# First stage of a two-layer hybrid trunk: the modulation beside the first column tiles, ordered anew

## The chip, the cores and the metric

The kernel runs on one core of one Trainium2 chip. The metric is the device time of an execution in microseconds (us), as a median over runs. Engines: TensorE (PE, its weight loads PEld), VectorE (DVE), ScalarE (ACT), GpSimd (POOL) and SyncE (SP), which issues nearly all loads.

## What is computed

A trunk of two layers over 256 latent and 256 context tokens of 2048 features. Only the entry of layer 0 matters here: a normalised input, modulated per feature, then projected.

```python
shift, scale, gate = jnp.split(jax.nn.silu(c) @ w_mod + b_mod, 3, axis=-1)
shift_x, scale_x, gate_x = jnp.split(jax.nn.silu(c_ctx) @ w_mod + b_mod, 3, axis=-1)
z_lat = (rms_norm(h_lat, norm_g) * (1.0 + scale[:, None]) + shift[:, None]) @ w_in
z_ctx = (rms_norm(h_ctx, norm_g) * (1.0 + scale_x) + shift_x) @ w_in
```

Everything is float32. The branches behind `z` (a gated linear recurrence, a gated delta rule, attention), the output projection and layer 1 follow, and the change leaves them as they are.

## The kernel before, in words

Activations lie as 16 feature tiles `Y` of 128 features by 512 tokens. A projection is exact to about float32: each operand is split into a high and a low float32r part (`xh`, `xl` of the input, `wh`, `wl` of the weights), and every contraction step makes three products of 128 x 512 (`accumulate`, lines 391 to 395).

The first stage is `start_layer` (line 528) for layer 0. It keeps seven column tiles (`FIRST`) open in seven PSUM tiles `pz`, `pz`, `pa`, `pa`, `pb`, `pb`, `pt`, and goes through the 16 feature tiles as contraction steps: 21 products a step. Before feature tile k can be used, its shift and scale must be known. They come from `mod_narrow` (lines 218 to 249), a generator. For a feature tile it goes through eight chunks of 128 x 512 weights of `w_mod0`: four load by themselves into `wb`, `wb`, `wa`, `wb`, four in pairs into `full` (or, every second tile, `th`) and `kq`. A chunk is four products of a stationary operand of two columns (`cs`, the SiLU of the two conditions), each in a column group of 32 of its own (`tile_position`), summed over the chunks in `pm`. Then ScalarE copies `pm` into `s`, TensorE transposes it, and VectorE adds up two column groups each, with the bias, into `modS` and `modA`, and applies the gain (`scale_gain`): a copy and three instructions. `modulate` (line 336) then makes `u`, `xh` and `xl` of the tile, in two halves of 256 tokens (latent and context).

The generator is pulled by `advance` (line 535): 8 steps beside the sums of squares (`rms_bcast`), one, then `LEAD` = 14 steps ahead of the first product, and one or two behind each column tile of a step. Each pull that uses a chunk also issues its load on SP's queue.

```python
for i in sorted(range(NSTART), key=lambda i: wide(TILES[l][i][0])):
    wh, wl = first_w[k][i // 4]
    accumulate(first[i], wh, wl, P * (i % 4), k, TT if wide(TILES[l][i][0]) else T)
    advance(1 + (i in (1, 5)))
```

The code's order is not the built order: a scheduler places the instructions of each engine by its own account of when their operands are there. All loads wait in SP's queue, in order; `wb` has 8 buffers, `wa` and `kq` 4 and 2, `full` and `th` one each, raw weights `wraw` and their parts `wh`, `wl` four each. Names in the trace are those of the tiles; nearly all computation has line 90, where a helper records it.

Of the kernel before, what the change touches and what calls it, by code (L numbers as in the profile page):

```python
# [7 lines left out]
F32 = mybir.dt.float32  # L8
# [13 lines left out]
# column tiles of the input projection, 128 columns each, in the order they are computed  # L22
# [14 lines left out]
LEAD = 14  # L37
# [14 lines left out]
class Timed:  # L52
    """An engine, with a rough account of when the work given to it will be done."""
# [42 lines left out]
def trunk(ctx, tc, xT, cT, consts, masks, rope_t, small, fg, w_mod0, w_mod, w_first, w_in, w_ba, w_rg, w_out, out):  # L96
# [31 lines left out]
    nc.sync.dma_start(out=cst[:, 0:C_TRI], in_=consts[:, 0:C_TRI])  # L128
    ident = cst[:, C_ID:C_ID + P]
# [32 lines left out]

    sm = []
    for l in range(2):
        s = big.tile([P, S_END], F32, name=f"small{l}")
        sm.append(s)
    nc.sync.dma_start(out=sm[0], in_=small[0])
# [50 lines left out]
    def mod_narrow():  # L218
        """Shift and scale of layer 0, one tile of features after the other; yields None, or the tile that is done."""
        pm = psum("pm", bufs=1)  # L220
        dve.memset(pm, 0.0)
        for u in range(KT):
            o = T * (u % 2)
            for j in range(8):
                if j < 4:
                    wm = tmp("wa" if j == 2 else "wb")
                    nc.sync.dma_start(out=wm, in_=w_mod0[u, j])
                else:
                    if j % 2 == 0:
                        tag = "kq" if j == 6 else ("full", "th")[u % 2]  # L230
                        two = tmp(tag, (P, 2, TT), bufs=BUFS.get(tag, 1))
                        nc.sync.dma_start(out=two, in_=w_mod0[u, j:j + 2].rearrange("j p c -> p j c"))
                    wm = two[:, j % 2]
# [3 lines left out]
                if j < 7:  # L237
                    yield None
            mt = tmp("s", (P, P))
            act.copy(out=mt, in_=pm[:, o:o + P])  # L240
            yield None
# [18 lines left out]
    def mod_step(engine=None):  # L260
        """One chunk of 256 x 512 weights: products on TensorE, or sums on VectorE with TensorE at the end."""
# [93 lines left out]
    def split(a, hi=None, lo=None):  # L355
        """The two float32r parts of a, in tiles of their own if no place is given."""
# [7 lines left out]
    def product3(out, a, b):  # L364
        """out = a.T @ b of two split operands."""
# [3 lines left out]
    class Weights:  # L369
        """Quarters (four of the sixteen contraction steps) of column tiles, in the order of their use."""  # L370
# [26 lines left out]
    def project(weights, ns, between):  # L397
        """One group of column tiles, with other work in between; returns their results in PSUM."""
# [28 lines left out]
    # depthwise convolution over the tokens of each segment; z in PSUM, token range [s0, s1) in halves  # L427
# [13 lines left out]
    # 2 silu(u), into dst  # L441
# [20 lines left out]
    class Background:  # L462
        """Lanes of work that runs between the projections, a step at a time, when its operands should be there."""
# [10 lines left out]
        def begin(self, makes, g):  # L474
            """The first step of a piece of work now, the others later."""
# [37 lines left out]
    def first_weights(l, k):  # L513
        raw = wp.tile([P, 1024], F32, tag="wraw", name="wraw", bufs=4)
        nc.sync.dma_start(out=raw[:, 0:P * NSTART], in_=w_first[l, k])
        first_w[k] = [split_w(raw[:, 0:512], 512), split_w(raw[:, 512:P * NSTART], P * NSTART - 512)]

    def gate_weights(l):
        """Columns of beta and alpha, split, of all contraction steps."""
# [8 lines left out]
    def start_layer(l, acc, bs, wide):  # L528
        """The layer's input, and with it, one contraction step after the other, its first column tiles."""
        first = [psum("pz"), psum("pz"), pa_(), pa_(), pb_(), pb_()]  # L530
        narrow = mod_narrow() if l == 0 else iter(())
        pr = rms_bcast(acc, TT, lambda: [mod_step(pe) if l else next(narrow, None) for _ in range(FILL if l else 8)])
        rb = tmp("wa")

        def advance(n):
            for _ in range(n):
                u = next(narrow, None)
                if u is not None:
                    modulate(l, u, rb)

        if l == 0:
            dve.tensor_copy(rb, pr)
            advance(1)
            first_weights(0, 0)
            advance(LEAD)
        else:
            modulate(l, 0, pr)
            dve.tensor_copy(rb, pr)
        first.append(pt_())
        for k in range(KT):  # L550
            if k + 1 < KT and k + 1 not in first_w:
                first_weights(l, k + 1)
            if l and k + 1 < KT:
                modulate(l, k + 1, rb)
            if l == 0 and k == 3:
                late_loads()
            for i in sorted(range(NSTART), key=lambda i: wide(TILES[l][i][0])):
                wh, wl = first_w[k][i // 4]
                accumulate(first[i], wh, wl, P * (i % 4), k, TT if wide(TILES[l][i][0]) else T)
                advance(1 + (i in (1, 5)))  # L560
# [3 lines left out]
    def layer(l, acc, bs):  # L564
# [8 lines left out]
        for dst, o in ((cq, 0), (sq_, T)):  # L573
            nc.sync.dma_start(out=dst, in_=rope_t[:, o:o + T])
            dve.tensor_scalar(out=dst, in0=dst, scalar1=s[:, S_QN:S_QN + 1], scalar2=None, op0=ALU.mult)
# [29 lines left out]
        def branch_result(k, src, cc, scale=None):  # L605
            """Columns cc of a branch's result, times half its gate if that is there."""
# [9 lines left out]
        def beta_alpha():  # L616
# [42 lines left out]
            # rows of the cumulated decay, to be read back on every partition  # L659
# [12 lines left out]
        # Keys stay as they come from the convolution; 1 / |k| of a token is carried by beta and v instead.  # L672
# [132 lines left out]
            # norm over the head's features, back to [feature, token]  # L805
# [414 lines left out]
```

## Time and profile before

| what | us |
|---|---|
| median of three runs (lowest, highest) | 1541.25 (1536.79, 1542.35) |
| span of the profiled execution (its own time is not listed beside it) | 1537.5 |
| TensorE busy | 1477.6 (96%) |
| VectorE busy | 1173.4 (76%) |
| ScalarE busy | 739.5 (48%) |
| three groups of products into `pz` | 642.5, 629.9, 629.8 |

The profile is one execution. Busy time of TensorE is that of pipelined products, whose ends are modelled, so starts that follow each other tell more than durations. In a row in order of time, the bracket behind an instruction is the idle time of its engine before it and what ended it. On TensorE and PEld a float32 product shows as two instructions, so a chunk of four products is x8.

### The profile page before, as it was taken

Reading aid. Unit: us, or ns where it says so; the run is one execution under the profiler, and the core shown is the slowest. Engines: PE = TensorE matmul, PEld = TensorE weight load, DVE = VectorE, ACT = ScalarE, POOL = GpSimd, SP = SyncE. Lnnn points to the kernel's source line nnn. Section 1 sums busy time; section 2 is a strip of 40 time slices with the busy share of each in tenths; the row PEclk is TensorE's granted clock in tenths of the full one; section 3 lists DMA queues with packets and bytes.
Section 4 is the critical chain, followed back from the end, with each engine's and each line's share of the span. In section 5 each row is a group of like instructions: output and inputs, shape, how many; then the busy total and the mean of one; then the engine's idle time right before and its main releaser. Section 6 shows DMA issues by size and latency. Waiting matters only on the chain.

```text
span 1537.5 us, 29960 instructions
## 1 busy us (share of the span) xinstructions
PE 1477.6 (96%) x11746; PEld 1200.2 (78%) x11746; DVE 1173.4 (76%) x2542; ACT 739.5 (48%) x1708; POOL 112.9 (7%) x114
## 2 busy tenths in 40 slices
PE   4999999999999999999999999999999999999996
PEld 2666768787877877788878887867977889779996
DVE  4444989898898898999748876787895676788755
ACT  3223445554444546655422224554644555677653
POOL 0000010100020010000011110010100100000011
PEclk9999999999999999999999998999999999999998
DMA  9996444343443463344436555544551333233553
GB/s 341 341 337 239 152 131 138 113 161 111 144 158 110 142 185 109 108 146 156 142 124 223 201 198 191 179 141 164 197 180 63 97 111 105 79 107 125 191 187 116
DMA packets 90686, 247.68 MB, mean 161 GB/s; under 512 B 9200, under 2 KB 20912, under 8 KB 90544
## 3 DMA queue, kind: packets, MB, share of 16 engines
q1 hardware_dynamic: 89392, 244.71, 47.7%
q8 instruction: 92, 1.51, 0.4%
q10 hardware_dynamic: 1152, 1.05, 0.2%
q14 instruction: 50, 0.41, 0.1%
HBM read 243.60 MB, written 2.13 MB: 160 GB/s over the span
## 4 chain that ended last, share of the span: by engine, by line
PE 80%; DVE 10%; DMA 4%; ACT 3%; issue 1%; POOL 1%; SPq 0%; DVEq 0%; POOLq 0%; ACTq 0%
PE pz L90 56%; PE pa L90 9%; PE pb L90 8%; PE pt L90 4%; PE pm L90 3%; DVE wb L90 2%; DVE wl L90 2%; DVE macc L90 1%; DVE th L90 1%; DMA wraw<-in_w_in 1%; DMA wa<-rows_d 1%; ACT wb L90 1%; DMA Y<-in_xT 1%; DVE u L90 1%; ACT t L90 1%
## 5 line engine op out<-in xcount | busy, mean ns | idle before, releaser
L90 PE MATMUL pz<-xh,wh 128*128 128x512 f32 (+1 forms) x1760 | 642.5, 367 | 1.7 <-ACT xh L90 1.7
L90 PE MATMUL pz<-xh,wl 128*128 128x512 f32 (+1 forms) x1760 | 629.9, 358 | 0.8 <-DVE wl L90 0.8
L90 PE MATMUL pz<-xl,wh 128*128 128x512 f32 (+1 forms) x1760 | 629.8, 358 | 0.0
L90 ACT CAST wh<-wraw 128x512 fp32r<-128x512 f32 x488 | 293.3, 612 | 335.8 <-PE pz L90 206.3
L90 DVE TENSOR_TENSOR wl<-wraw,wh 128x512 fp32r<-128x512 f32 x488 | 329.4, 683 | 135.7 <-ACT wh L90 133.4
L90 PEld LDWEIGHTS pz<-xl,wh 128*128 128x128 f32 x1760 | 331.8, 189 | 50.0 <-issue 3.1
L90 PEld LDWEIGHTS pz<-xh,wh 128*128 128x128 f32 x1760 | 331.9, 189 | 48.9 <-ACT xh L90 2.4
L90 PEld LDWEIGHTS pz<-xh,wl 128*128 128x128 f32 x1760 | 332.3, 189 | 42.4 <-DVE wl L90 1.2
L90 DVE SCALAR_TENSOR_TENSOR macc<-wm,cs,macc 128x512 f32<-128x512 f32 x400 | 293.3, 766 | 1.4 <-DMA wm<-in_w_mod 1.0
L90 PE MATMUL pb<-wb 128*128 128x128 f32 (+1 forms) x560 | 112.6, 328 | 3.6 <-ACT wb L90 1.9
L90 PEld LDWEIGHTS pb<-wb 128*128 128x128 f32 x560 | 79.6, 190 | 16.7 <-ACT wb L90 6.9
L90 POOL TENSOR_TENSOR o<-o,t 128x512 f32<-128x512 f32 (+1 forms) x28 | 30.5, 1091 | 326.2 <-ACT t L90 326.2
L90 ACT ACTIVATE wb<-pb,mx,rqa 128x512 f32<-128x512 f32 (+1 forms) x48 | 33.9, 707 | 42.6 <-DVE mx L90 42.3
L90 DVE SCALAR_TENSOR_TENSOR u<-zp,small,u 128x512 f32<-128x512 f32 (+1 forms) x72 | 50.6, 702 | 1.9 <-ACT u L90 1.7
L90 DVE COPY s<-pm 128x64 f32<-128x64 f32 x16 | 3.6, 225 | 62.5 <-PE pm L90 62.5
L90 ACT ACTIVATE xh<-u,modS 128x256 fp32r<-128x256 f32 x64 | 29.3, 502 | 45.1 <-DVE u L90 45.0
L90 ACT ACTIVATE t<-pt 128x128 f32<-128x128 f32 (+1 forms) x122 | 34.1, 280 | 32.0 <-PE pt L90 29.9
L90 PEld LDWEIGHTS pa<-c,s 32*32 32x32 f32 x2304 | 25.0, 107 | 21.7 <-issue 12.0
L90 ACT COPY s<-pm 128x128 f32<-128x128 f32 x16 | 4.3, 267 | 70.5 <-PE pm L90 70.5
L90 DVE TENSOR_REDUCE mx<-pb 128x1 f32<-128x512 f32 (+1 forms) x48 | 28.7, 599 | 10.3 <-PE pb L90 9.9
L90 POOL TENSOR_TENSOR rqa<-rqa,mhalf 128x4 f32<-128x4 f32 (+1 forms) x16 | 17.3, 1084 | 244.7 <-DVE rqa L90 244.7
L90 ACT COPY wb<-pb 128x512 f32<-128x512 f32 (+1 forms) x48 | 24.7, 515 | 21.7 <-PE pb L90 21.0
(259 smaller groups left out, 1812.7 us busy)
## 6 DMA issues: line engine op xcount, KB each, us to landing
wraw<-in_w_in SPq DMA_DIRECT2D x148, 512.0 KB, 3.6
wm<-in_w_mod SPq DMA_DIRECT2D x128, 512.0 KB, 3.6
wraw<-in_w_out SPq DMA_DIRECT2D x64, 512.0 KB, 4.2
wraw<-in_w_first SPq DMA_DIRECT2D x32, 448.0 KB, 4.6
wb<-in_w_mod SPq DMA_DIRECT2D x48, 256.0 KB, 5.6
kq<-in_w_mod SPq DMA_DIRECT2D x16, 512.0 KB, 5.1
Y<-in_xT SPq DMA_DIRECT2D x16, 256.0 KB, 5.3
wa<-in_w_mod SPq DMA_DIRECT2D x16, 256.0 KB, 5.7
```

The lines of the kernel that those rows point to most:

```text
L90: return f(*args, **kw)
```

## The change

`mod_narrow` becomes a class `Narrow` with three parts: `load` issues all six loads of a tile, `run` makes four of its chunks (after the second four also the copy to `s`), and `end` makes the sums. In `end` one product with a selection matrix `sel4` (128 x 4, a sum of columns of the identity) takes the place of the transposition, and two VectorE instructions with two scalars each write `modA` and `modS`. `pm` uses its first 128 columns for every tile.

`start_layer` for layer 0 becomes `start_first`. In the code, the second four chunks of tile k+1 stand behind the second column tile of step k, its sums behind the third, and the first four chunks of tile k+2 behind the sixth. Loads are issued as whole tiles, three steps ahead. The small parameters load ahead of `Y`; masks, the rope tables, the weights of beta and alpha and other small blocks (`late`) load in step 11 instead of the beginning and step 3. Layer 1 keeps its code.

```diff
@@ small parameters ahead of Y, the selection matrix
+    sm = [big.tile([P, S_END], F32, name=f"small{l}") for l in range(2)]
+    nc.sync.dma_start(out=sm[0], in_=small[0])
...
+    sel4 = big.tile([P, 4], F32, name="sel4")
+    for g in range(2):
+        dve.tensor_tensor(out=sel4[:, 2 * g:2 * g + 2], in0=ident[:, 32 * g:32 * g + 2], in1=ident[:, 64 + 32 * g:66 + 32 * g], op=ALU.add)
@@ mod_narrow becomes Narrow
+        def run(self, u, half):
+            for j in range(4 * half, 4 * half + 4):
                 for c in range(4):
-                    pe.matmul(out=pm[32 * c:32 * c + 2, o:o + P], lhsT=cs[:, 2 * j + c // 2, :], rhs=wm[:, c * P:c * P + P],
+                    pe.matmul(out=self.pm[32 * c:32 * c + 2, 0:P], lhsT=cs[:, 2 * j + c // 2, :], rhs=self.chunks[u][j][:, c * P:c * P + P],
                               start=(j == 0), stop=(j == 7), tile_position=(0, 32 * c))
...
-            pe.transpose(out=pm[:, o + P:o + 2 * P], in_=mt, identity=ident)
-            even = tmp("s", (P, P))
-            dve.tensor_copy(even[:, 0:64], pm[:, o + P:o + P + 64])
-            for g, dst in enumerate((modS[0], modA[0])):
-                dve.scalar_tensor_tensor(out=dst[:, u, :], in0=pm[:, o + P + 64 + 32 * g:o + P + 66 + 32 * g], scalar=sm[0][:, S_BM + 16 * g + u:S_BM + 16 * g + u + 1],
-                                         in1=even[:, 32 * g:32 * g + 2], op0=ALU.add, op1=ALU.add)
-            scale_gain(0, u, 1)
-            yield u
...
+        def end(self, u):
+            pe.matmul(out=self.pm[:, 0:4], lhsT=self.mt, rhs=sel4, start=True, stop=True)
+            dve.tensor_scalar(out=modA[0][:, u, :], in0=self.pm[:, 2:4], scalar1=self.one[:, u:u + 1], scalar2=sm[0][:, S_G + u:S_G + u + 1], op0=ALU.add, op1=ALU.mult)
+            dve.tensor_scalar(out=modS[0][:, u, :], in0=self.pm[:, 0:2], scalar1=sm[0][:, S_BM + u:S_BM + u + 1], scalar2=None, op0=ALU.add)
@@ start_first
+        for u in range(2):
+            narrow.load(u)
+            first_load(0, u)
+        pr = rms_bcast(acc, TT, lambda: narrow.run(0, 0))
+        rb = tmp("wa")
+        dve.tensor_copy(rb, pr)
+        narrow.run(0, 1)
+        narrow.end(0)
+        modulate(0, 0, rb)
+        first_split(0)
...
+        for k in range(KT):
+            for i in range(NSTART):
+                wh, wl = first_w[k][i // 4]
+                accumulate(first[i], wh, wl, P * (i % 4), k, TT)
+                if k + 1 == KT:
+                    continue
+                if k == 0 and i == 0:
+                    narrow.run(1, 0)
+                if i == 1:
+                    narrow.run(k + 1, 1)
+                    if k + 3 == KT - 1:
+                        first_load(0, k + 3)
+                    if k + 3 < KT:
+                        narrow.load(k + 3)
+                    if k + 3 < KT - 1:
+                        first_load(0, k + 3)
+                    first_split(k + 1)
+                if i == 2:
+                    narrow.end(k + 1)
+                    modulate(0, k + 1, rb)
+                if i == 5 and k + 2 < KT:
+                    narrow.run(k + 2, 0)
+            first_w.pop(k)
+            if k == KT - 5:
+                late()
```

The first place is TensorE in step 1, around the sums for tile 2 (`cst,s` is the transposition, `sel4,s` the selection product; `xh1`, `xl1` are the operand of step 1, `xh2` that of step 2). Before:

```order
L90 MATMUL pm_240<-kq_432,cs_107 2x128 x8
L90 MATMUL pz_222<-xl1_374,wh_414 128x512
L90 MATMUL pz_223<-xh1_373,wl_415 128x512
L90 MATMUL pm_240<-cst_71,s_442 128x128
L90 MATMUL pz_223<-xl1_374,wh_414 128x512
L90 MATMUL pa_224<-xh1_373,wl_415 128x512
L90 MATMUL pa_224<-xl1_374,wh_414 128x512
L90 MATMUL pa_225<-xh1_373,wl_415 128x512
L90 MATMUL pm_240<-wb_465,cs_107 2x128 x4
```

and now, from the selection product to the first product of step 2:

```order
L89 MATMUL pm_222<-sel4_121,s_469 128x4
L89 MATMUL pb_221<-xh1_411,wh_400 128x512
L89 MATMUL pb_221<-xh1_411,wl_401 128x512
L89 MATMUL pb_221<-xl1_412,wh_400 128x512
L89 MATMUL pt_341<-xh1_411,wh_400 128x512
L89 MATMUL pt_341<-xh1_411,wl_401 128x512
L89 MATMUL pm_222<-wb_382,cs_110 2x128 x4
L89 MATMUL pt_341<-xl1_412,wh_400 128x512
L89 MATMUL pm_222<-wb_384,cs_110 2x128 x4
L89 MATMUL pm_222<-wa_386,cs_110 2x128 x4
L89 MATMUL pz_216<-xh2_500,wh_485 128x512
```

Before, ten more products and the rest of tile 3's chunks up to the `th` pair follow until step 2; now the sums stand six products, and two pieces of the next tile's chunks, ahead of it.

The second place is VectorE between two tiles' sums. Before:

```order
L90 COPY s_540<-pm_240 128x64
L90 SCALAR_TENSOR_TENSOR modS0_127<-pm_240,small0_124,s_540 128x2
L90 SCALAR_TENSOR_TENSOR modA0_131<-pm_240,small0_124,s_540 128x2
L90 SCALAR_TENSOR_TENSOR modA0_131<-modA0_131,small0_124 128x2
L90 SCALAR_TENSOR_TENSOR u_545<-Y3_81,modA0_131,wa_293 128x256 x2
L90 SCALAR_TENSOR_TENSOR xl3_547<-u_545,modS0_127,xh3_546 128x256 x2
L90 TENSOR_TENSOR wl_599<-wraw_596,wh_598 128x512
L90 TENSOR_TENSOR wl_603<-wraw_596,wh_602 128x384
```

and now, for tile 3:

```order
L89 TENSOR_SCALAR modA0_134<-pm_222,nb_224,small0_73 128x2
L89 TENSOR_SCALAR modS0_130<-pm_222,small0_73 128x2
L89 SCALAR_TENSOR_TENSOR u_588<-Y3_84,modA0_134,wa_287 128x256
L89 TENSOR_TENSOR wl_575<-wraw_394,wh_574 128x512
L89 TENSOR_TENSOR wl_579<-wraw_394,wh_578 128x384
L89 SCALAR_TENSOR_TENSOR u_588<-Y3_84,modA0_134,wa_287 128x256
L89 SCALAR_TENSOR_TENSOR xl3_590<-u_588,modS0_130,xh3_589 128x256 x2
```

The two halves of `u` followed each other; now the two splits of the weights stand between them (in tiles 1 to 4, 6, 7, 9, 10, 12 and 13).

The third place is TensorE where tile 15's sums are made. Before, in step 14 (`xh14`):

```order
L90 MATMUL pm_240<-kq_1632,cs_107 2x128 x8
L90 MATMUL pz_222<-xl14_1563,wh_1614 128x512
L90 MATMUL pz_223<-xh14_1562,wl_1615 128x512
L90 MATMUL pm_240<-cst_71,s_1642 128x128
L90 MATMUL pz_223<-xl14_1563,wh_1614 128x512
```

and now, at the end of step 14:

```order
L89 MATMUL pm_222<-wb_1465,cs_110 2x128 x4
L89 MATMUL pt_341<-xh14_1567,wh_1556 128x512
L89 MATMUL pt_341<-xh14_1567,wl_1557 128x512
L89 MATMUL pm_222<-wb_1467,cs_110 2x128 x4
L89 MATMUL pt_341<-xl14_1568,wh_1556 128x512
L89 MATMUL pm_222<-wa_1469,cs_110 2x128 x4
L89 MATMUL pm_222<-wb_1471,cs_110 2x128 x4
L89 MATMUL pm_222<-th_1473,cs_110 2x128 x8
L89 MATMUL pm_222<-kq_1475,cs_110 2x128 x8
L89 MATMUL pm_222<-sel4_121,s_1625 128x4
L89 MATMUL pz_216<-xh15_1642,wh_1627 128x512
```

Before, 14 products of step 14 followed the transposition; now all of step 14 stands ahead of the selection product, and step 15 directly behind it.

## Rows read from the trace of the kernel before

**Rows 1.** Stretches: us, busy us (instructions) per engine, clock, DMA share, GB/s.

```profile
33.00:38.00 5.00, 5.00 (x35) 2.88 (x34) 0.00 (x0) 0.00 (x0) 0.00 (x0) 0.66 1.02 370
...
100.00:120.00 20.00, 20.00 (x230) 12.51 (x230) 9.63 (x28) 5.71 (x14) 0.00 (x0) 1.00 0.96 334
```

**Rows 2.** TensorE in order of time, one step: start, us, instruction, idle before.

```profile
110.24 0.62 PE L90 MATMUL pm<-wb,cs 128*2 128x128 f32 x16
110.67 0.40 PE L90 MATMUL pm<-wa,cs 128*2 128x128 f32 x8
...
115.64 0.40 PE L90 MATMUL pz<-xh,wl 128*128 128x512 f32 x1
115.96 0.62 PE L90 MATMUL pm<-kq,cs 128*2 128x128 f32 x16
...
116.85 0.40 PE L90 MATMUL pz<-xh,wl 128*128 128x512 f32 x1
117.09 0.27 PE L90 MATMUL pm<-cst,s 128*128 128x128 f32 x1
117.11 0.48 PE L90 MATMUL pz<-xl,wh 128*128 128x512 f32 x1
117.43 0.39 PE L90 MATMUL pa<-xh,wl 128*128 128x512 f32 x1
...
118.22 0.62 PE L90 MATMUL pm<-wb,cs 128*2 128x128 f32 x16
```

**Rows 3.** All engines in order of time, the start of the stage.

```profile
11.53 0.33 SPq L167 DMA_DIRECT2D small<-in_small  x1
...
26.28 0.69 DVE L90 COPY wa<-pt 128x512 f32<-128x512 f32 x1 [1.23 <-PE pt L90]
...
28.67 0.33 PE L90 MATMUL pm<-cst,s 128*128 128x128 f32 x1 [0.40 <-ACT s L90]
...
32.25 0.50 PE L90 MATMUL pz<-xh,wh 128*128 128x512 f32 x1 [1.72 <-ACT xh L90]
```

**Rows 4.** TensorE in order of time, the end of the stage.

```profile
152.83 0.39 PE L90 MATMUL pz<-xh,wl 128*128 128x512 f32 x1
...
157.50 0.40 PE L90 MATMUL pz<-xh,wh 128*128 128x512 f32 x1
```

**Rows 5.** TensorE in order of time, sums of squares ahead of layer 1.

```profile
930.17 0.37 PE L90 MATMUL pt<-cst,o 128*128 128x2 f32 x2
930.39 0.36 PE L90 MATMUL pt<-cst,kv 128*128 128x2 f32 x2
```

**Rows 6.** VectorE, ScalarE, VectorE again in order of time: the operand's chain.

```profile
117.39 0.23 DVE L90 COPY s<-pm 128x64 f32<-128x64 f32 x1 [4.02 <-PE pm L90]
...
117.79 0.21 DVE L90 SCALAR_TENSOR_TENSOR modA<-pm,small,s 128x2 f32<-128x2 f32 x1
118.04 0.16 DVE L90 SCALAR_TENSOR_TENSOR modA<-modA,small 128x2 f32<-128x2 f32 x1
118.23 0.88 DVE L90 SCALAR_TENSOR_TENSOR u<-Y,modA,wa 128x256 f32<-128x256 f32 x2
...
118.75 0.91 ACT L90 ACTIVATE xh<-u,modS 128x256 fp32r<-128x256 f32 x2 [1.84 <-DVE u L90]
...
149.88 0.68 DVE L90 TENSOR_TENSOR wl<-wraw,wh 128x512 fp32r<-128x512 f32 x1
...
150.48 0.15 DVE L90 SCALAR_TENSOR_TENSOR modA<-modA,small 128x2 f32<-128x2 f32 x1
150.55 0.55 DVE L90 TENSOR_TENSOR wl<-wraw,wh 128x384 fp32r<-128x384 f32 x1
151.01 0.88 DVE L90 SCALAR_TENSOR_TENSOR u<-Y,modA,wa 128x256 f32<-128x256 f32 x2
151.81 0.69 DVE L90 TENSOR_TENSOR wl<-wraw,wh 128x512 fp32r<-128x512 f32 x1
```

**Rows 7.** The page, costliest groups: busy us, mean ns of one, idle before.

```profile
L90 ACT ACTIVATE xh<-u,modS 128x256 fp32r<-128x256 f32 x64 | 29.3, 502 | 45.1 <-DVE u L90 45.0
```

More of the change, by code (lines that the diff above doesn't have):

```diff
@@ L35 @@
 HOLD = 2
-LEAD = 14
 FILL = 6
@@ L161, in trunk @@
     dve.tensor_scalar(out=cs, in0=ctt, scalar1=0.5, scalar2=None, op0=ALU.mult)
[L163 to L167, printed above, removed]
     def late_loads():
@@ L216, in scale_gain, with __init__, load @@
             in1=sm[l][:, S_G + k0:S_G + k0 + n].unsqueeze(2).to_broadcast([P, n, 2]), op0=ALU.add, op1=ALU.mult)
[L218 to L233, printed above, removed]
+    class Narrow:
+        def __init__(self):
+            self.pm = psum("pm", bufs=1)
+            dve.memset(self.pm, 0.0)
+            self.one = big.tile([P, KT], F32, tag="nb", name="nb")
+            dve.tensor_scalar(out=self.one, in0=sm[0][:, S_BM + 16:S_BM + 32], scalar1=1.0, scalar2=None, op0=ALU.add)
+            self.chunks = {}
+        def load(self, u):
+            w = []
+            for j in range(4):
+                wm = tmp("wa" if j == 2 else "wb")
+                nc.sync.dma_start(out=wm, in_=w_mod0[u, j])
+                w.append(wm)
+            for j in (4, 6):
+                tag = "kq" if j == 6 else ("full", "th")[u % 2]
+                two = tmp(tag, (P, 2, TT), bufs=BUFS.get(tag, 1))
+                nc.sync.dma_start(out=two, in_=w_mod0[u, j:j + 2].rearrange("j p c -> p j c"))
+                w += [two[:, 0], two[:, 1]]
+            self.chunks[u] = w
+        def run(self, u, half):
+            for j in range(4 * half, 4 * half + 4):
@@ L234, in mod_narrow @@
                 for c in range(4):
-                    pe.matmul(out=pm[32 * c:32 * c + 2, o:o + P], lhsT=cs[:, 2 * j + c // 2, :], rhs=wm[:, c * P:c * P + P],
+                    pe.matmul(out=self.pm[32 * c:32 * c + 2, 0:P], lhsT=cs[:, 2 * j + c // 2, :], rhs=self.chunks[u][j][:, c * P:c * P + P],
                               start=(j == 0), stop=(j == 7), tile_position=(0, 32 * c))
[L237 to L240, printed above, removed]
@@ L248, in mod_narrow @@
-            scale_gain(0, u, 1)
-            yield u
+            if half:
+                self.mt = tmp("s", (P, P))
+                act.copy(out=self.mt, in_=self.pm[:, 0:P])
+                self.chunks.pop(u)
+        def end(self, u):
+            pe.matmul(out=self.pm[:, 0:4], lhsT=self.mt, rhs=sel4, start=True, stop=True)
+            dve.tensor_scalar(out=modA[0][:, u, :], in0=self.pm[:, 2:4], scalar1=self.one[:, u:u + 1], scalar2=sm[0][:, S_G + u:S_G + u + 1], op0=ALU.add, op1=ALU.mult)
+            dve.tensor_scalar(out=modS[0][:, u, :], in0=self.pm[:, 0:2], scalar1=sm[0][:, S_BM + u:S_BM + u + 1], scalar2=None, op0=ALU.add)
@@ L511, in trunk, with first_load, first_split @@
     first_w = {}
+    first_raw = {}
+    def first_load(l, k):
+        first_raw[k] = wp.tile([P, 1024], F32, tag="wraw", name="wraw", bufs=4)
+        nc.sync.dma_start(out=first_raw[k][:, 0:P * NSTART], in_=w_first[l, k])
+    def first_split(k):
+        raw = first_raw.pop(k)
+        first_w[k] = [split_w(raw[:, 0:512], 512), split_w(raw[:, 512:P * NSTART], P * NSTART - 512)]
     def first_weights(l, k):
-        raw = wp.tile([P, 1024], F32, tag="wraw", name="wraw", bufs=4)
-        nc.sync.dma_start(out=raw[:, 0:P * NSTART], in_=w_first[l, k])
-        first_w[k] = [split_w(raw[:, 0:512], 512), split_w(raw[:, 512:P * NSTART], P * NSTART - 512)]
+        first_load(l, k)
+        first_split(k)
     def gate_weights(l):
@@ L526, in gate_weights, with start_first @@
         return bs
+    def start_first(acc, late):
+        first = [psum("pz"), psum("pz"), pa_(), pa_(), pb_(), pb_()]
+        narrow = Narrow()
+        for u in range(2):
[8 more added lines that the diff above has]
+        first_split(0)
+        narrow.load(2)
+        first_load(0, 2)
+        first.append(pt_())
+        for k in range(KT):
[23 more added lines that the diff above has]
+                late()
+        return first
@@ L528, in start_layer @@
     def start_layer(l, acc, bs, wide):
         first = [psum("pz"), psum("pz"), pa_(), pa_(), pb_(), pb_()]
-        narrow = mod_narrow() if l == 0 else iter(())
-        pr = rms_bcast(acc, TT, lambda: [mod_step(pe) if l else next(narrow, None) for _ in range(FILL if l else 8)])
+        pr = rms_bcast(acc, TT, lambda: [mod_step(pe) for _ in range(FILL)])
         rb = tmp("wa")
[L535 to L548, printed above, removed]
+        modulate(l, 0, pr)
+        dve.tensor_copy(rb, pr)
         first.append(pt_())
         for k in range(KT):
-            if k + 1 < KT and k + 1 not in first_w:
+            if k + 1 < KT:
                 first_weights(l, k + 1)
-            if l and k + 1 < KT:
@@ L554, in start_layer @@
                 modulate(l, k + 1, rb)
-            if l == 0 and k == 3:
-                late_loads()
             for i in sorted(range(NSTART), key=lambda i: wide(TILES[l][i][0])):
@@ L572, in layer, with rope_tables @@
         sq_ = big.tile([P, T], F32, tag="sq", name="sq")
-        for dst, o in ((cq, 0), (sq_, T)):
-            nc.sync.dma_start(out=dst, in_=rope_t[:, o:o + T])
-            dve.tensor_scalar(out=dst, in0=dst, scalar1=s[:, S_QN:S_QN + 1], scalar2=None, op0=ALU.mult)
+        def rope_tables():
+            for dst, o in ((cq, 0), (sq_, T)):
+                nc.sync.dma_start(out=dst, in_=rope_t[:, o:o + T])
+                dve.tensor_scalar(out=dst, in0=dst, scalar1=s[:, S_QN:S_QN + 1], scalar2=None, op0=ALU.mult)
         sp = big.tile([P, 8], F32, tag="sp", name="sp")
@@ L1081, in layer, with late @@
         wide = lambda kind: not last or kind in ("gk", "gv", "xa", "kc", "vc")
-        first = start_layer(l, acc, bs, wide)
+        def late():
+            nonlocal bs
+            late_loads()
+            rope_tables()
+            bs = gate_weights(0)
+        if last:
+            rope_tables()
+            first = start_layer(l, acc, bs, wide)
+        else:
+            first = start_first(acc, late)
         tiles = TILES[l][NSTART:]
@@ L1129, in trunk @@
         square_into(acc, Y[k], k, TT, dve)
-    gw = [gate_weights(0)]
-    acc = layer(0, acc, gw[0])
+    gw = []
+    acc = layer(0, acc, None)
     mod_finish(((1, 0), (1, 1)))
-    acc = layer(1, acc, gw[1])
+    acc = layer(1, acc, gw[0])
     pr = rms_bcast(acc, T)
```

2 lines of the change are left out of this document (removed).

## The prediction

> **What bounds the kernel now.** I read the busy time by stretches first. The stage that the change rewrites is the first: the modulation of layer 0 beside the first seven column tiles. In a stretch of its steady part TensorE is busy all 20 us at full clock while the transfers use 0.96 of the DMA engines [rows 1], so both are near their end; which of them is it? The instructions of one step on TensorE in order of time answer that [rows 2]. A step is the work of one feature tile: 21 products of 512 columns, eight chunks of the modulation (128 columns, four column groups) and one transposition. The first run of chunks of one step starts at 110.24, that of the next at 118.22: 7.98 us, and inside it every gap is that of the instruction stream, none a wait for a load. The stage goes from the first product at 32.25 [rows 3] to the first product of the next column tile at 157.50 [rows 4]: 125.25 us. After it nothing is changed but the places of a few instructions, and TensorE stays busy, so I take it that what this stage loses or gains reaches the end whole.
>
> **The prices of TensorE.** Products of 512 columns follow at (157.50 - 152.83) / 20 = 0.2335 us [rows 4]. Chunks inside a run follow at (110.67 - 110.24) / 2 = 0.2135 [rows 2]. From the product at 115.64 to that at 116.85 lie two products' time and a run of two chunks: 1.21 - 2 x 0.2335 - 2 x 0.2135 = 0.31 is what the run costs beyond its chunks [rows 2]. The transposition: 117.43 - 116.85 - 2 x 0.2335 = 0.11. Check by the step, which has four runs: 4.90 + 1.71 + 4 x 0.31 + 0.11 = 7.96, against 7.98. Check by the stage: 336 products 78.46, 117 chunks 24.98 (11 are ahead of it), 58 runs 17.98, 15 transpositions 1.65: 123.07. The other 2.2 us lie mostly in the first step, where the mean clock from 33 to 38 is 0.66: 3.4 of those 5 us at 1.2 GHz, half of the full clock, which costs 1.7 [rows 1]. I keep that remainder.
>
> **Runs and selection product: +5.9 us.** The code speaks of two runs of four chunks per tile. The built order does not have them: each step holds a run of two (the pair `full` or `th`), one of two (`kq`), and the other four chunks in two or three pieces among products. From the first product on I count 71 runs for 58, and 118 chunks for 117: 13 x 0.31 + 0.21 = 4.2. By the Trainium skill, TensorEngine Tiling (Array Packing), section Key Properties, a change of tiling mode drains TensorE; the 0.31 per run agrees, and without such a drain these 13 runs would cost nothing and the stage would end 4 us sooner. The selection product takes the transposition's place. Its stationary operand is the same 128 x 128 block, but it takes two passes. The nearest row is the product with 2 columns at full clock, (930.39 - 930.17) = 0.22 us each [rows 5]; below it stands the transposition's 0.11. I take 0.22: 15 x 0.11 = 1.7. Together +5.9 us.
>
> **One step ahead: +6.5 us.** This is the wait that the change adds. In the kernel before, the transposition of tile k+1 is the eighth of a step's 21 places, so the operand that follows from it has 14 products and two runs of time. Now the selection product stands after 14 to 17 of the 21, and the next step's first product is queued behind it on TensorE. What must happen in between is read from VectorE's and ScalarE's rows of the same step [rows 6]. The transposition starts at 117.09, VectorE takes its result at 117.39: 0.30, and 0.11 more for a second pass. Then modA; a result used by the next instruction comes 118.04 - 117.79 = 0.25 later, and with modS put in I take 0.28. The first half of u starts at 0.69 after the selection product. VectorE's next instruction starts 0.60 after a wl of 512, 0.46 after one of 384, 0.40 after half a u (151.01 to 151.81 for two halves, which end after 0.88). ScalarE's xh takes 0.50 per half [rows 7], and starts 0.05 after its u. For 10 of the 15 tiles VectorE's order is now u, wl, wl, u. The second half of u then starts at 0.69 + 0.40 + 0.60 + 0.46 = 2.15 and ends 0.48 later, xh is there at 3.18, and the product can start 0.05 later: 3.23 after the selection product. For tiles 5, 8, 11, 14 and 15 both halves of u come first: 1.06 less, 2.17.
>
> What TensorE has to do from the selection product on, 0.24 us after the product ahead of it [rows 2]: where 15 products are done, six more and runs of one and two: 7 x 0.2335 + 0.22 + 2 x 0.31 + 3 x 0.2135 - 0.24 = 2.87, so 0.36 of waiting (steps 1, 3, 6, 9, 12: 1.8). Where 17 are done and a run of three follows: 2.10, waiting 1.13 (steps 5, 8, 11: 3.4). Step 0, with 16 done: 2.33, waiting 0.90. Step 2, with 14: 3.11, waiting 0.12. Steps 4, 7 and 10 prepare tiles 5, 8 and 11: 2.9 against 2.17, none. Step 13 has no more chunks behind it: 1.85 against 2.17, 0.32. Sum 6.5 us. The bounds: nothing if the chain is always as short as for tile 5 except in steps 0 and 13, and 10 if each link is a tenth longer.
>
> **The end of the stage: +2.5 us.** The last tile's chunks and its selection product stand behind all products of step 14. From the start of the `kq` chunks, ScalarE's copy and the way to the product take 117.09 - 115.96 = 1.13 [rows 2], where TensorE alone would need 0.43 + 0.12; then 2.17 until the operand is there, where it would need 0.22. So 0.58 + 1.95 = 2.5 us.
>
> **The start: -0.3 us.** From the transposition of tile 0 at 28.67 to the first product at 32.25 are 3.58 us [rows 3]. Now: modA at 0.41, modS and the copy of the 1/rms to `wa` behind it, 0.13 + 0.60 + 0.20 (the copy was long done before, at 26.28, and now stands behind modA in VectorE's queue), two halves of u 0.88, xh 0.55 and 0.05: 2.82, so 0.75 sooner. Against that, the small parameters now load ahead of Y, one issue of 0.33 and its gap [rows 3], and everything up to the sums of squares waits for Y: 0.45 later. The four transfers that moved behind the stage's middle (masks, rope, beta and alpha) are 1 us of transfer time beside a chain of VectorE and TensorE, so they bring nothing at the start; the bounds here are -1.5 and +0.5. VectorE's two instructions per tile in place of four lie beside TensorE's work and shorten only the chain costed above.
>
> **Sum.** 5.9 + 6.5 + 2.5 - 0.3 = +14.6 us. The profiled execution spans 1537.5 us; it stands 3.75 below the median of the runs, 1541.25, and nothing around it is listed. I forecast **1556 us** as a median (1552 as a span), slower by 0.95%. A measurement here can tell about 0.5% from no change, 7.7 us.
>
> **Rivals.**
> *The chain is short enough.* If VectorE runs the two halves of u in time, the waits inside the steps vanish: 5.9 + 2.5 - 0.3 = 8.1, 1549 us, at the edge of no change. For it: 117.39 to the end of xh at 119.66 is only 2.3 us now [rows 6]. Against it: two wl, 1.06 us, now stand between the halves. 0.2.
> *The clock falls.* The five waits of 0.9 us and more (steps 0, 5, 8, 11 and the end) are followed by a stretch at 1.2 GHz, as the idle 1.72 us ahead of 32.25 were [rows 1, 3]: 1.7 us each, up to +8.5, 1564 us. Against it: that idle time stood behind several others. 0.1. The Trainium skill, TensorE: Matmul & The Clock Gate, section on HAM oscillation, tells of a kernel whose waits between groups of products sent the clock down each time; no row of the steady stage shows that.
> *The price of a run is a wait for its buffers, not a change of tiling* (ends on the other side). Each run's first instruction waits for a load's semaphore; loads now stand two tiles ahead in the order of use. If a run then cost only a third of 0.31, 71 runs would give back 71 x 0.21 = 15 us and the kernel would be no slower; at nothing it would be 22 us, and 1534. It decides at a price under 0.11. Against it: the 0.31 is the same for runs of one, two and three chunks with one, one and three buffers, and half of it lies behind the run. 0.07.
>
> **How the numbers follow.** Forecast 0.63, rivals 0.2, 0.1, 0.07. Of the first rival half falls within 0.5%, of the last most is faster; a twentieth of the forecast's own cases has smaller waits and joins no change. Faster 0.05, same 0.17, slower 0.78. The range, 1546 to 1563, holds the forecast with its bounds, most of the first rival, and nearly all of the second.
>
> **What would show it.** In the profile after: the first product near 32.0; chunks of `kq` some 8.8 us apart instead of 7.98, uneven between 8.4 and 9.5; idle time of TensorE before `pz<-xh,wh` released by ScalarE's xh, once per step, 1.1 us in steps 5, 8 and 11; about 3 us idle ahead of the last tile's first product; the next column tile at 172. If `kq` chunks follow at 8.4, the first rival is right; at under 8, the last; if the granted clock dips in the stage, the second. A stage as predicted with another total would mean that what follows the stage has changed, which I hold to be unmoved.

## The result and the profile after

The changed kernel takes 1554.11 us (median of 4 runs, 1552.67 to 1556.28), the kernel before 1540.28 us beside it (4 runs): ratio 1.0092, 95% interval 1.0075 to 1.0108, slower by 0.9%. The forecast was 1556 us and slower. The profiled execution spans 1550.9 us for 1537.5.

All of that lies in the first stage, and more than all of it. TensorE's rows of the changed kernel in order of time (start, us, instruction, idle before it) show the start, one step, the end of the stage, and two landmarks of layer 1:

```profile
29.86 0.39 PE L89 MATMUL pm<-sel,s 128*128 128x4 f32 x2 [0.38 <-DMA wb<-in_w_mod]
...
32.68 0.53 PE L89 MATMUL pz<-xh,wh 128*128 128x512 f32 x1 [0.71 <-ACT xh L89]
...
111.03 0.40 PE L89 MATMUL pb<-xh,wl 128*128 128x512 f32 x1
111.26 0.28 PE L89 MATMUL pm<-sel,s 128*128 128x4 f32 x2
111.40 0.48 PE L89 MATMUL pb<-xl,wh 128*128 128x512 f32 x1
111.72 0.40 PE L89 MATMUL pt<-xh,wh 128*128 128x512 f32 x1
...
114.44 0.51 PE L89 MATMUL pz<-xh,wh 128*128 128x512 f32 x1 [1.09 <-ACT xh L89]
...
164.60 0.62 PE L89 MATMUL pm<-kq,cs 128*2 128x128 f32 x16
165.61 0.38 PE L89 MATMUL pm<-sel,s 128*128 128x4 f32 x2 [0.38 <-ACT s L89]
167.82 0.50 PE L89 MATMUL pz<-xh,wh 128*128 128x512 f32 x1 [1.83 <-ACT xh L89]
...
172.80 0.40 PE L89 MATMUL pz<-xh,wh 128*128 128x512 f32 x1
...
945.95 0.37 PE L89 MATMUL pt<-cst,o 128*128 128x2 f32 x2
...
953.59 0.39 PE L89 MATMUL pa<-xh,wh 128*128 128x256 f32 x1 [0.57 <-ACT xh L89]
```

The stage goes from the first product, 32.68 (32.25 before [rows 3]), to the next column tile, 172.80 (157.50 [rows 4]): 140.12 us for 125.25, +14.87. The sum of the prediction for the stage was +14.9. A step is longer in threes: the selection products follow each other at 8.8, 8.6 and 9.4 us, where the transpositions before came every 7.99.

The chain behind that selection product, on VectorE and ScalarE in order of time, answers to [rows 6]:

```profile
111.58 0.28 DVE L89 TENSOR_SCALAR modA<-pm,nb,small 128x2 f32<-128x2 f32 x1 [6.31 <-PE pm L89]
...
111.91 0.48 DVE L89 SCALAR_TENSOR_TENSOR u<-Y,modA,wa 128x256 f32<-128x256 f32 x1
...
112.30 1.16 DVE L89 TENSOR_TENSOR wl<-wraw,wh 128x512 fp32r<-128x512 f32 x2
...
113.37 0.48 DVE L89 SCALAR_TENSOR_TENSOR u<-Y,modA,wa 128x256 f32<-128x256 f32 x1
...
113.88 0.51 ACT L89 ACTIVATE xh<-u,modS 128x256 fp32r<-128x256 f32 x1 [0.96 <-DVE u L89]
```

111.26 to 114.44 is 3.18 us, where TensorE had 2.1 us to do: 1.09 of idle time. TensorE's waits from 33 to 173 us (what for, us in all, times, longest) have one name, but for 0.4 us at the end; before, there was none behind the first product. Of the 8.4 us, 0.7 lie ahead of the stage's first product (32.68 above), 1.8 at the end and 5.9 in the steps between:

```profile
PE pz L89 <- ACT xh L89: 8.4, 11, 1.8
PE pm L89 <- ACT s L89: 0.4, 1, 0.4
```

The granted clock is no part of these 14.87 us: in the same stretches as [rows 1] (columns: busy us of PE, PEld, DVE, ACT and POOL, granted clock, DMA share, GB/s) it is 0.66 at the start, as before, and 1.00 in the steady part. The DMA share has fallen from 0.96 to 0.83, because the steps are longer. The last line is layer 1's start, for what follows:

```profile
33.00:38.00 5.00, 5.00 (x42) 2.15 (x40) 0.94 (x3) 0.00 (x0) 0.00 (x0) 0.66 0.93 346
100.00:120.00 20.00, 18.91 (x197) 11.06 (x196) 6.20 (x16) 4.70 (x12) 0.00 (x0) 1.00 0.83 282
946.00:956.00 10.00, 9.43 (x121) 7.30 (x120) 3.68 (x11) 1.70 (x4) 1.02 (x1) 0.83 0.71 258
```

At the end of the stage the kernel is 15.3 us behind, at the end of the span 13.4. The missing 1.9 us come back in layer 1, in stretches at another clock: at its sums of squares it is still 15.8 behind (945.95 for 930.17 [rows 5]); at its first product 14.5, since TensorE ran more of the way there at 1.2 GHz in the execution profiled before than in this one. Before, that product and the ten microseconds around it:

```profile
939.08 0.38 PE L90 MATMUL pa<-xh,wh 128*128 128x256 f32 x1 [0.36 <-ACT xh L90]
```

```profile
930.00:940.00 10.00, 9.64 (x105) 7.06 (x98) 2.38 (x8) 0.91 (x2) 1.02 (x1) 0.66 0.66 245
```

The changed kernel did the same work from 946 to 956 at 0.83, the last of the three lines above. The remaining 1.1 us lie behind that product; from 1028 to 1036 us the kernel before was granted 0.79, the changed kernel 1.00 at the same place, 1042 to 1050. Such stretches differ between executions of one kernel: 21 executions of the kernel before span 1533.9 us at a mean clock of 0.996 to 1540.3 at 0.990. So in what follows a term is read from the stage, where it can be located, and the medians are the check.

### The profile page after: what moved, and what is told of

Its sections match the earlier page's. It is cut to its first block, busy times and chain, and to the rows that moved or that the text cites. A ratio compares the mean times of both kernels' runs of the same rounds, so it can differ in the third digit from the quotient of the medians.

```text
span 1550.9 us, 29964 instructions
## 1 busy us (share of the span) xinstructions
PE 1482.8 (96%) x11762; PEld 1197.9 (77%) x11762; DVE 1164.5 (75%) x2513; ACT 739.3 (48%) x1708; POOL 112.2 (7%) x114
## 4 chain that ended last, share of the span: by engine, by line
PE 76%; DVE 13%; DMA 4%; ACT 4%; issue 2%; POOL 1%; SPq 0%; DVEq 0%; ACTq 0%; POOLq 0%
PE pz L89 54%; PE pa L89 9%; PE pb L89 7%; PE pt L89 3%; PE pm L89 3%; DVE wl L89 3%; DVE wb L89 2%; DVE macc L89 2%; DMA wraw<-in_w_in 1%; DVE u L89 1%; DVE th L89 1%; DMA wb<-in_w_mod 1%; ACT wb L89 1%; ACT wh L89 1%; DMA Y<-in_xT 1%
## 5 line engine op out<-in xcount | busy, mean ns | idle before, releaser
L89 DVE TENSOR_SCALAR modA<-pm,nb,small 128x2 f32<-128x2 f32 x16 | 4.5, 279 | 92.5 <-PE pm L89 92.5
```

What stands on the lines that cost most here:

```text
L89: return f(*args, **kw)
```

## Experiments

The first three take the change's own terms apart. In them (and in the fifth to ninth) TensorE's order in the stage is written out: A to U are the 21 products of a step, c is a chunk, * the selection product, or the transposition in the kernels made from the one before. Edges between neighbours of that list fix the order in which the engine is given its instructions and wait for nothing.

**1. VectorE's order.**

```diff
-                    modulate(0, k + 1, rb)
+                    for low, ins in zip(lows[-2:], modulate(0, k + 1, rb)):
+                        behind(low, ins)
```

`lows` holds the instructions wl; `modulate` now gives back its last u and its last xl.

> The kernel after with TensorE's order in the stage kept instruction by instruction; on VectorE both halves of u now stand ahead of the first wl of each tile, and xl ahead of the second. My theory (the waits of the steps come from the order u, wl, wl, u on VectorE): xh is there 2.1 us after the selection product for every tile, as it already is for tiles 5, 8, 11, 14 and 15, against a cover of 2.1 to 2.9 us, so of the 6.6 us that TensorE waits for xh inside the steps about 0.5 stays (step 13); runs, end of the stage and start stay. Stage 140.1 - 6.1 = 134.0 us, time 1554.1 - 6.1 = 1548, ratio to the kernel before 1.005. Rival (the idle time only shows there, and what is late is a load or the wl of the same tile): the wait moves to another operand, under 2 us come back, 1552 or more.

Measured: 1549.14 us (4 runs), ratio 1.0064, interval 1.0043 to 1.0084. TensorE in order of time, first and last selection product, last tile, next column tile:

```profile
29.42 0.39 PE L108 MATMUL pm<-sel,s 128*128 128x4 f32 x2 [0.40 <-ACT s L108]
...
158.63 0.39 PE L108 MATMUL pm<-sel,s 128*128 128x4 f32 x2 [0.39 <-ACT s L108]
160.85 0.50 PE L108 MATMUL pz<-xh,wh 128*128 128x512 f32 x1 [1.83 <-ACT xh L108]
...
167.38 0.40 PE L108 MATMUL pz<-xh,wh 128*128 128x512 f32 x1
```

From the first selection product to the last it is 129.21 us for 135.75: -6.5, where 6.1 were expected; of 8.4 us of waiting for xh 2.5 are left, 1.8 of them at the end and 0.7 ahead of the stage's first product, and none in the steps. The stage became only 5.0 us shorter, because the last tile took 8.75 us from its selection product on for 7.19: behind the idle 1.83 us the clock fell.

```profile
161.00:164.00 3.00, 3.00 (x9) 2.36 (x10) 2.80 (x6) 1.61 (x3) 0.00 (x0) 0.64 0.25 48
```

So the waits of the steps are VectorE's order, and the rival is out. The rival "the clock falls" of the prediction is not wrong either: it did so here, at the one wait that is left, for 1.56 us, and had not in the profiled execution of the changed kernel.

**2. Runs of four.** Two of the sixteen lines of the list:

```diff
-    "cccABcCDEFGHccIJKLMccNO*PQRSTcU"
-    "ccABcCDEFGHccIJKLccMN*OPQRScTU"
+    "ccccABCDEFGHIJKLMccccNO*PQRSTU"
+    "ccccABCDEFGHIJKLccccMN*OPQRSTU"
```

> The kernel after with its chunks gathered: between two selection products one run of four at the end of the step and one of four two products ahead of the selection product, eight in one run ahead of the last; products and selection products stand where they stood. From the first product on 31 runs in place of 71, the same chunks. My theory (0.31 us for each change between runs and products): -40 x 0.31 = -12.4 us; the waits for xh change by under 1 us in sum (0.46 for 0.36 in five steps, 0.92 for 1.13 in three). Stage 127.7 +- 1 us, time 1541.7, ratio 1.001. Rival (the price of a run is a wait for its buffers): a run of four waits as long in one piece as its pieces did, the stage stays within 3 us of 140.1 and the time at 1551 or more; or more waits for transfers appear on the chunks.

Measured: 1541.10 us (10 runs), ratio 1.0011, interval 0.9999 to 1.0023: from 0.9% slower to no change.

```profile
29.80 0.39 PE L108 MATMUL pm<-sel,s 128*128 128x4 f32 x2 [0.39 <-DMA wb<-in_w_mod]
...
153.06 0.39 PE L108 MATMUL pm<-sel,s 128*128 128x4 f32 x2 [0.38 <-ACT s L108]
155.28 0.50 PE L108 MATMUL pz<-xh,wh 128*128 128x512 f32 x1 [1.83 <-ACT xh L108]
...
161.80 0.40 PE L108 MATMUL pz<-xh,wh 128*128 128x512 f32 x1
```

Between the first and the last selection product: 123.26 us for 135.75, -12.49 for 40 runs, 0.31 each. The waits for xh that are listed in the steps went from 5.9 to 5.3 us beside it; if all of that is taken off, 0.30 are left. Behind the stage's first product no wait for a load appears. Again the last tile ran in part at the lower clock (0.53 from 155.5 to 158), 8.74 us for 7.19, so the stage lost 10.9 in all. The price of a run is that of changing between chunks and products; waiting for buffers has no part in it that these rows show.

**3. The order of the code.** The code states two runs of four per step and a selection product after nine products; the scheduler had built something else. Here the list is what the code says:

```diff
-    "cccABcCDEFGHccIJKLMccNO*PQRSTcU"
+    "ABCDEFccccGHI*JKLMNOPQRccccSTU"
```

> The kernel after with TensorE's instructions of the stage in the order in which the code states them: 6 products, a run of four, 3 products, selection product, 9 products, a run of four, 3 products. 30 runs from the first product on for 71, and 12 products and a run of four behind each selection product. My theory: runs -41 x 0.31 = -12.7; cover behind the selection product 12 x 0.2335 + 0.31 + 0.85 + 0.22 = 4.2 us against a chain of 3.2, so the 6.6 us of waits in the steps go; the last tile's sums are long done, so 2.5 us at the end go. -21.8: stage 118.3 us, time 1532, ratio 0.995. If the three terms are right but the transfers cannot follow (2.556 MB a step at 349 GB/s, which the kernel before's 341 GB/s at a share of 0.97 gives, is 7.3 us against 7.45 of TensorE), waits for loads show on the chunks and up to 4 us of it are lost, 1536. Rival (runs cost waits for buffers): the chunks stand up to nine products earlier than in the kernel after, so the waits for loads grow, and the time is 1545 or more.

Measured: 1533.88 us (6 runs), ratio 0.9973, interval 0.9959 to 0.9988: the same change, 20 us faster than as it was built, and faster than the kernel before. One step, and the start:

```profile
29.18 0.39 PE L108 MATMUL pm<-sel,s 128*128 128x4 f32 x2 [0.40 <-ACT s L108]
32.00 0.80 PE L108 MATMUL pz<-xh,wh 128*128 128x512 f32 x1 [2.43 <-ACT xh L108]
...
84.12 0.28 PE L108 MATMUL pm<-sel,s 128*128 128x4 f32 x2
...
91.59 0.28 PE L108 MATMUL pm<-sel,s 128*128 128x4 f32 x2
...
151.75 0.39 PE L108 MATMUL pz<-xh,wh 128*128 128x512 f32 x1
```

Every step is 7.46 or 7.47 us against 7.45 of the sum, and TensorE waits for nothing after its first product. The stage is 119.75 us, 20.4 less than the changed kernel's, for 21.8 expected: the rest lies at its start, where TensorE, idle for 2.43 us with no chunks to run, was at 1.2 GHz until 38 us.

```profile
32.00:35.00 3.00, 3.00 (x31) 1.77 (x35) 1.26 (x4) 0.00 (x0) 0.00 (x0) 0.50 1.04 388
```

**4. The kernel before with runs of four.** The generator loads a tile's eight chunks first and takes each four in reverse order, which keeps a run together in the built order.

```diff
-            for j in range(8):
+            for n, j in enumerate((3, 2, 1, 0, 7, 6, 5, 4)):
```

> The kernel before with one part of the change alone: each tile's chunks in two runs of four (29 runs from the first product on for 58); transposition, lead of two tiles and everything else as before. My theory: -29 x 0.31 = -9.0 us, a step of 4.90 + 1.71 + 0.62 + 0.11 = 7.34 for 7.98, if the transfers can follow (share 0.96 before, 7.3 us a step at full use): 1531 to 1536, ratio 0.994 to 0.997. Rival (the price of a run is a wait for its buffers): the time stays within 2 us of 1540.

Measured: 1537.18 us (10 runs), ratio 0.9991, interval 0.9980 to 1.0003: hardly anything, as the rival had it, but not for its reason. The runs are gone (28 in the trace, 30 fewer), yet three steps take 23.45 us, 7.82 each for 7.34. The whole stage is 124.09 us for 125.25. TensorE and ScalarE in order of time, where one step ends and the next begins:

```profile
90.84 0.49 PE L90 MATMUL pt<-xl,wh 128*128 128x512 f32 x1
...
90.97 0.27 ACT L90 COPY s<-pm 128x128 f32<-128x128 f32 x1 [3.88 <-PE pm L90]
...
91.14 1.03 ACT L90 CAST wh<-wraw 128x512 fp32r<-128x512 f32 x2
...
91.29 0.33 PE L90 MATMUL pm<-cst,s 128*128 128x128 f32 x1
...
91.81 0.50 PE L90 MATMUL pz<-xh,wh 128*128 128x512 f32 x1 [0.19 <-ACT wh L90]
```

In most steps the new order has only one product, or none, between the run and the transposition (in one step of three it has three), so that TensorE waits for ScalarE's copy; and there the transposition stands at the end of the step, so that the casts of the next step's weights, queued behind that copy, come too late for its first product. A new wait took the place of the runs: this experiment did not isolate what it was to isolate.

**5. The same with the kernel before's own order.**

```diff
-    "ADGJBccCE*FHIKcccLcMNOPQRccSTU"
+    "ADGJBccccCE*FHIKLccccMNOPQRSTU"
```

> The kernel before with its chunks gathered into two runs of four per step and the transposition left at its eighth place: 5 products, a run of four, 2 products, the transposition, 5 products, a run of four, 9 products. The run of four of the fourth experiment stood one product ahead of the transposition, whose wait for ScalarE's copy (0.4 us a step) and the casts queued behind that copy took back what the runs gave; here two products stand between. 29 runs from the first product on for 58. My theory (0.31 us a run): step 4.90 + 1.71 + 0.62 + 0.11 = 7.34 for 7.98, stage 125.25 - 9.0 = 116.3 us, time 1538.2 - 9.0 = 1529, ratio 0.994. Rival (in the fourth experiment it was the transfers that held the steps at 7.8 us): the step stays at 7.7 or more, the stage over 121 us, with waits for loads at the chunks, and the time over 1534.

Measured: 1529.10 us (4 runs), ratio 0.9941, interval 0.9924 to 0.9957. The list has 30 runs from the first product on, 28 fewer, where the expectation counted 29. Each transposition of the steady part stands 7.35 to 7.38 us behind the one before it. The end of a run and what stands behind it:

```profile
103.17 0.62 PE L109 MATMUL pm<-kq,cs 128*2 128x128 f32 x16
103.72 0.50 PE L109 MATMUL pz<-xl,wh 128*128 128x512 f32 x1
104.06 0.40 PE L109 MATMUL pz<-xh,wl 128*128 128x512 f32 x1
104.29 0.27 PE L109 MATMUL pm<-cst,s 128*128 128x128 f32 x1
```

The stage is 116.89 us for 116.3 expected. That is 8.36 us for 28 runs, 0.30 each. With two products in between, no wait for the copy: the price of a run holds in the kernel before too.

**6. One run of eight.**

```diff
-    "ADGJBccccCE*FHIKLccccMNOPQRSTU"
+    "ADGJBccccccccCE*FHIKLMNOPQRSTU"
```

> As the experiment before, but all eight chunks of a tile in one run: 5 products, a run of eight, 2 products, the transposition, 14 products. 15 runs from the first product on. My theory: TensorE's step is 4.90 + 1.71 + 0.31 + 0.11 = 7.03 us, but 2.556 MB at the 350 GB/s that the third experiment shows at a share of 0.99 to 1.00 is 7.30 us: so waits for loads appear at the chunks, the step is 7.3 to 7.4 as soon as the tiles loaded ahead are used up, and the stage lies between 112 (TensorE alone) and 116.5 us; time 1525 to 1529. Rival (the transfers do not bind yet): no wait for loads, step 7.03, stage 112, time 1524.5. If the price of a run was a matter of its length, the stage does not move from that of two runs.

Measured: 1529.48 us (4 runs), ratio 0.9941, interval 0.9923 to 0.9959. Steps of 7.06 us, a stage of 112.23: the stage that the rival gave, and no wait for a load (one of 1.48 us for a cast of weights, at 41.30, is the only one listed behind the first product). My limit for the transfers was wrong: they moved 388 GB/s.

```profile
60.00:80.00 20.00, 20.00 (x254) 15.61 (x253) 10.65 (x30) 6.11 (x15) 0.00 (x0) 1.00 1.04 388
```

The median does not show the 4.7 us that the stage gained on the fifth experiment; the ninth returns to that.

**7. The change with one run of eight.**

```diff
-    "ABCDEFccccGHI*JKLMNOPQRccccSTU"
+    "ABCDEFccccccccGHI*JKLMNOPQRSTU"
```

> The kernel after in the order of its code, with one run of eight in place of two of four: 6 products, a run of eight, 3 products, the selection product, 12 products. Behind the selection product 12 products: 12 x 0.2335 + 0.22 = 3.0 us against the chain of 3.2 (order u, wl, wl, u) or 2.2, so up to 0.2 us of wait comes back in some steps. TensorE's step 4.90 + 1.71 + 0.31 + 0.22 = 7.14, under the 7.30 of the transfers. My theory: stage 119.75 less 0 to 4.6 us, bounded by the transfers to about 117.5; time 1531.5, ratio 0.996. Rival (the chain binds again): 0.2 us and more of wait for xh in every step, nothing gained on the third experiment, 1534.

Measured: 1532.51 us (4 runs), ratio 0.9957, interval 0.9940 to 0.9973; stage 119.03. The rival was right: every step takes 7.48 to 7.50 us, and TensorE waits for no load.

```profile
85.05 0.28 PE L108 MATMUL pm<-sel,s 128*128 128x4 f32 x2
...
87.82 0.39 PE L108 MATMUL pt<-xl,wh 128*128 128x512 f32 x1
88.23 0.51 PE L108 MATMUL pz<-xh,wh 128*128 128x512 f32 x1
```

The last product of the step starts at 87.82 and would be followed at 88.05; the next step's first starts at 88.23, 3.18 behind the selection product, the length of the chain to the hundredth. The view of the waits does not list so short a one.

**8. The same with the first experiment's order on VectorE.** The edit is that of the first experiment.

> The kernel of the seventh experiment (the change, in the order of its code, with one run of eight) with the order of the first on VectorE: u, u, wl, xl, xl, wl. There the step was 7.50 us where TensorE's work is 7.14, because the first product starts 3.18 us behind the selection product, the length of the chain with u, wl, wl, u. My theory: with both u first the chain is 2.1 us, under the 3.0 of the 12 products, so the step falls to 7.14 and the stage from 119.0 by 14 x 0.36 = 5.0 to 114; time 1532.5 - 5 = 1527.5, ratio 0.9925. Rival (the transfers hold the step near 7.3 to 7.5 and the chain only shows it): the step stays at 7.3 or more, with waits for loads at the chunks; 1530 or more.

Measured: 1528.99 us (6 runs), ratio 0.9920, interval 0.9899 to 0.9941. Steps of 7.15 us for 7.14, a stage of 114.22 for 114:

```profile
89.77 0.28 PE L108 MATMUL pm<-sel,s 128*128 128x4 f32 x2
...
96.92 0.28 PE L108 MATMUL pm<-sel,s 128*128 128x4 f32 x2
...
147.74 0.39 PE L108 MATMUL pz<-xh,wh 128*128 128x512 f32 x1
```

This is the change's idea with its three terms taken out, its median 25 us under that of the kernel as it was built, and 0.8% faster than the kernel before.

**9. The sixth once more.**

> The kernel of the sixth experiment once more, with more runs: its stage was 4.7 us shorter than that of the fifth, its median 0.4 us longer, with four runs each whose mean clocks lay between 0.990 and 0.997. My theory: at the same mean clock it is 4 us faster than the fifth kernel, and with as many runs as this the ratio is 0.991 to 0.993. Rival (the faster stage is paid back behind it, in layer 1's start or elsewhere): the ratio stays at 0.994 or more, and the span behind the stage is 4 us longer than the 1380 us of the kernel before.

Measured: 1530.55 us (6 runs), ratio 0.9931, interval 0.9907 to 0.9954; stage 113.68, and 1529.9 - 146.43 = 1383.5 us behind it at a mean clock of 0.990, where the sixth experiment's profile has 1379.6 at 0.995 and the kernel before 1380.0. The ratio is at the upper edge of what my theory gave, the interval reaches past the rival's 0.994, and the span behind the stage is nearly the rival's in this profile. But the sixth experiment's profile is one of the same kernel with the same short steps, and has 3.9 us less behind the stage: in these two the length behind the stage follows the execution, not the stage. That all of the 4.7 us arrives is not shown by the medians.

## Why the prediction was right

The total was right (+14.6 forecast, +13.8 between the medians), and the three terms of the stage, which make +14.9 of it, came out each by itself. Two smaller parts were off, the start by +0.7 us and what reaches the end by -1.9; that they have opposite signs is luck.

- **Runs and selection product, +5.9.** 13 more runs at 0.31: the second experiment gives 12.49 / 40 = 0.31 a run (0.30 with its waits taken off), the third (7.46 - 4.90 - 1.71 - 0.22) / 2 = 0.315. The selection product: from 111.03 to 111.72 lie two products and it, 0.69 - 0.467 = 0.22, the value taken from the nearest row [rows 5]. The rule of the Trainium skill, TensorEngine Tiling (Array Packing), section Key Properties, that a change of mode drains TensorE, agrees with the 0.31 that is paid per change and not per chunk. That it is the mode is not shown: chunks and products also differ in type, float32 and float32r. The selection product, float32 as well but on the whole array, costs 0.22 us in all, so a change of type alone cannot make up the 0.31.
- **One step ahead, +6.5.** The first experiment, which changes VectorE's order and nothing else, takes 6.54 us out between the first selection product and the last. Single waits are listed as 0.88 in step 0 (0.90 forecast), 0.32 to 0.35 where 0.36 was forecast, 1.09 and 1.10 where 1.13 was. The list adds up to 5.9 only, because it counts from the modelled end of the product before and leaves short waits out: in step 13 (0.32 forecast) two products start 0.50 apart, at 156.94 and 157.44, where 0.23 is usual, and no wait is listed. The chain was 3.18 for 3.23; modA started 0.32 behind the selection product and not 0.41, and took longer itself, 0.28.
- **The end, +2.5.** From the `kq` chunks (164.60) to the last tile's first product (167.82) 3.22 us, less 0.77 of TensorE's own work: 2.45.
- **The start, -0.3.** +0.43 instead. The chain from the selection product to the first product was forecast at 2.82 and is 2.82, here and in the first and third experiments. What the term left out is TensorE's rate ahead of that. The selection product of tile 0 was to stand 0.45 behind the 28.67 of the transposition, at 29.12, and stands at 29.86. The `kq` chunks ahead of it, here and in the third experiment:

```profile
28.40 1.08 PE L89 MATMUL pm<-kq,cs 128*2 128x128 f32 x16
...
28.18 0.61 PE L108 MATMUL pm<-kq,cs 128*2 128x128 f32 x16
```

The pair `full` ahead of them starts at 27.59 here and at 27.60 there, in the same order. From it to the selection product it is 2.27 us here, 1.58 there, and in the kernel before 1.44 to the transposition (27.23 to 28.67). Two chunks take 0.43 us at full clock [rows 2], but the pair `full` took 0.81 here: about half the rate, as at 1.2 GHz. That it is the clock is inferred from these rates. The granted clock is listed as 1.00 from 20 to 30 us in all three, but it is listed so around 20 us too, where products of two columns follow at 0.43 us and not at the 0.22 of [rows 5].

- **"What this stage loses reaches the end whole"** is the sentence that failed: 15.3 us were lost, 13.4 arrived in the two profiles. The stretches at 1.2 GHz behind the stage fell otherwise in the two executions compared. Over all eleven profiles the part behind the stage takes 1375.2 to 1383.5 us, and not in the order of the stages: 1378.1 behind the longest, of 140.1 us, and 1379.6, 1383.5 and 1380.7 behind the three of 112 to 114.

Of the rivals, "the chain is short enough" would have needed the order that the first experiment builds; "the clock falls" was right in kind and price (1.7 forecast, 1.56 and 1.55 measured) at the last wait in two kernels of three that have it, and did not come at the waits inside the steps; "the price of a run is a wait for its buffers" is refuted by the second and fifth experiments. The Trainium skill, TensorE: Matmul & The Clock Gate, section on HAM oscillation, tells of waits for loads, of some 3 to 5 us, between groups of products that send the clock down each time. The waits of 0.3 to 1.1 us in these steps, which are shorter, left it at 1.00.

## What to carry to other kernels

A change of order is what the scheduler builds of it, not what the code says: the same code was 0.9% slower than the kernel before as built, and 0.3% faster in the order that it states. Read the built order, count the changes between kinds of matmul (0.31 us each here) and, at each dependency that crosses engines, compare the chain with the work that stands behind it in the queue; both numbers come from rows of the kernel that one already has. When one piece is put in another place to test a price, look first at what waits in the new place.

## What was not expected

- The transfers were thought to be near their limit, 349 GB/s at full share, from a share of 0.97 at 341. They moved 388 GB/s at a listed share of 1.04 and followed steps of 7.06 us, which the limit would have held at 7.3: the share is no distance to a ceiling. [rows 1] had said so, with 370 GB/s at 1.02. The Trainium skill, DMA: Bandwidth & Descriptors, section Specifications, gives 435 GB/s as the ceiling of the fabric and about 358 GB/s as one core's limit at the HBM. The 388 GB/s here, with one core running the kernel, are under the first and above the second.
- The same idle 1.83 us ahead of the last tile left the clock at 1.00 in one profiled execution and brought it to 0.53 and 0.64 for some microseconds in two others.
